# Turned query and key rows split once over 128 partitions, and raw weight quarters held in tiles of the exponentials

## The chip, the cores and the metric

The kernel runs on one core of a Trainium2 chip. The metric is the device time of one execution in microseconds, as the median of several runs. The engines of a core work side by side, each through its own queue in order: TensorE (PE, matmuls and transpositions into PSUM banks), VectorE (DVE), ScalarE (ACT), GpSimd (POOL), and SyncE (SP), which here issues nearly all DMAs. The profile shows one execution.

## The reference

It is one decoder layer on 1024 tokens of width 1024 in float32. One normalised input goes through one projection, whose columns feed two groups of heads. Cut to what matters here:

```
h = rms_norm(x, norm1_w)
da_q, da_k, da_v, dn_qkv, dn_z, dn_a, dn_b = split(h @ w_in)
da_q, da_k = rms_norm(da_q, q_norm_w), rms_norm(da_k, k_norm_w)   # rows of 64
# differential attention, 4 heads, two 64-wide maps per head
a = softmax(q1 k1^T / 8) - lam * softmax(q2 k2^T / 8)             # causal
da_o = rms_norm(a @ v) * (1 - lam_init)
dn_o = rms_norm(gated_delta_rule(conv_silu(dn_qkv), ...)) * silu(dn_z)   # the "scan"
x = x + concat(da_o, dn_o) @ w_out
x = x + relu(rms_norm(x, norm2_w) @ w_up)**2 @ w_down
```

The change touches the projection of `da_q`, `da_k` and `da_v`, and the way in which queries and keys reach the attention.

## The kernel before

**Matmuls in two parts.** A float32 operand is split into a high part, rounded to the format in which PE multiplies fast (`fp32r` in the profile), and a low part, which is the rest. A product is three matmuls: high by high, high by low, low by high. Every weight so passes through `load_unit` (L199 to L215): a DMA brings a raw piece into a tile `wraw` (L211), ACT casts it into the high part `wH` (L213), and another engine, here DVE, subtracts to get the low part `wL` (L214). There are two `wraw` tiles, and a raw tile is free for the next load when its subtraction is done.

**The attention's projection** (`da_units`, L987). The 1536 columns of `da_q`, `da_k` and `da_v` are projected as three *units* of 512 columns (`todo`). The first unit's weights are loaded elsewhere; those of units two and three by `half_w`, in two halves of four quarters each. A half holds 4 of the 8 blocks of 128 rows of the weight; a quarter is one such block, 128 x 512, which comes in two DMAs of 128 KB (two ranges of 256 columns). For each unit the kernel walks over the eight blocks of 128 tokens in pairs: 2 x 24 matmuls `ps_qk` (L1012 to L1014) into two PSUM banks of the pool `pj`, first those of the first half weight for both blocks, then those of the second. At the last pair of a unit, half the next unit's weights are asked for as soon as the matmuls of the first half are written, the other half after those of the second.

**Leaving the bank** (`leave`). ACT copies the finished bank to `qn` with a scale per token (L1040; for unit two in two pieces, L1034 for values and L1035). Only then can PE start on that bank again. POOL, DVE and POOL again form the norm of each row of 64, and DVE scales `qn` with it.

**Turns** (`da_turns`, L957). There are 32, one for each block of tokens and each 256 columns of queries or keys. PE transposes two blocks of 128 x 128 into a bank `ps_qkt` of the pool `px` (L966, L967), so that the two 64-wide maps of a head lie on partitions 0 to 63 and 64 to 127. Then for each of the two maps (`m`) ACT writes the high part of its 64 partitions (L972) and DVE the low part (L973) on the other 64 partitions of the tile `qa`, so that `qa[:, m]` holds both parts of one map over all 128 partitions. One DMA of 256 KB stores the tile to `qk_d` in DRAM (L977). The attention loads keys from there (`load_head`, two tiles `KS` a head) and queries (`load_q`, L1081), also with their halves exchanged (`qb`). The weights of the norms, `qw` and `kw`, scale the turned rows; the profile shows `kw` as `pv`.

**Attention.** For each head and block of queries, `scores` multiplies (L1148, `ps_sc`), takes the negated maximum (DVE, L1153) and the exponential (ACT, L1157) into a tile `pexp` of 128 x 1024, and combines the two maps on DVE (L1167). `values` transposes the result on PE into `ps_at` (L1189), ACT copies it (L1191), and PE multiplies by the values. Four `pexp` tiles stand in the pool `ae`; before the first exponential the same four hold `gb` and `pb` of the scan's preparation (`horner`). A third exponential of each three goes to a pool `be` once the scan is over.

**The scan** runs at the same time, with loads of `pka` (L839), `pkb` (L894) and `zgt` (L896), PE's `ps_A` (L875), and its output on DVE and ACT (L914, L919, L924). `sy` is its copy that PE waits for at L875.

**What sets the order.** All this is written by generators that a planner (`Interleave`, L40) runs by priority: each yields the time from which it can go on, or a bank. The planner keeps its own clock, which goes forward with the matmuls written (`flow.pe`), and a queue for each engine, in which `flow.chain` enters costs such as `act(256)` or `vec(256, 60)`. For a DMA it adds `DMA_T` = 2500 ns. `unit_time` (L771) gives the times at which the four quarters of a half are to be ready; the third and fourth start when the first and second are done:

```
for i in range(4):
    start = flow.now if i < 2 else done[i - 2]
    done.append(flow.chain(("S", 520.0), (eng, rate), start=start + DMA_T))
```

A store is written when the planner's clock has reached its data (`put_off`). The framework's own scheduler then places what is written in each engine's queue; a load whose tile is free early can stand there far ahead of its place in the code. So a changed cost or a changed tile moves other instructions, too.

Of the kernel before, what the change touches and what calls it, by code (L numbers as in the profile page):

```python
# [18 lines left out]
P = 128  # L19
SEQ = 1024  # L20
DM = 1024
KB = DM // P
NT = SEQ // P
# [5 lines left out]
UC = 260  # L29
# [103 lines left out]
def tile_hymba_layer(  # L133
# [6 lines left out]
    nc = tc.nc  # L140
    V, S, G, T = nc.vector, nc.scalar, nc.gpsimd, nc.tensor
# [3 lines left out]
    w_in_v = w_in[0].rearrange("(kb p) c -> p kb c", p=P)  # L145
# [5 lines left out]
    dram = ctx.enter_context(tc.tile_pool(name="dram", bufs=1, space=DRAM))  # L151
# [39 lines left out]
    qk_d = dram.tile([2, 2, NT, P, 2, 2, P], F32, name="qk_d")  # L191
# [4 lines left out]
    hH = hpool.tile([P, KB, SEQ], F32R, name="hH")  # L196
    hL = hpool.tile([P, KB, SEQ], F32R, name="hL")

    def load_unit(src, ranges, k0=0, nk=KB, eng=None, rp=None):  # L199
        eng = eng or G  # L200
        width = sum(n for _, n in ranges)
        wh, wl = staged("wH"), staged("wL")
        wh = wh[:, :nk * width].rearrange("p (k c) -> p k c", k=nk)
        wl = wl[:, :nk * width].rearrange("p (k c) -> p k c", k=nk)
        st = 2 * UC // width
        for k in range(0, nk, st):
            raw = rp.tile([P, 2 * UC], F32, tag="wraw", name="wraw", bufs=5) if rp else laid("wraw")
            raw = raw[:, :st * width].rearrange("p (k c) -> p k c", k=st)
            o = 0
            for c0, n in ranges:  # L210
                nc.sync.dma_start(raw[:, :, o:o + n], src[:, k0 + k:k0 + k + st, c0:c0 + n])  # L211
                o += n
            S.copy(wh[:, k:k + st, :], raw)  # L213
            eng.tensor_tensor(wl[:, k:k + st, :], raw, wh[:, k:k + st, :].bitcast(F32), ALU.subtract)  # L214
        return wh, wl  # L215
# [149 lines left out]
    with tc.manual_schedule(engines={T.engine, V.engine, S.engine}):  # L365
# [49 lines left out]
        raw = n1.tile([P, NT, UC], F32, name="zr")  # L415
# [331 lines left out]
    ae = actx.enter_context(tc.tile_pool(name="ae", bufs=4, **right))  # L747
# [16 lines left out]
    flow = Interleave()  # L764
# [3 lines left out]
    HF = (slice(0, 64), slice(64, 128))  # L768
    MM, TR = 219.0, 110.0

    def unit_time(eng="G", rate=1230.0):  # L771
        done = []
        for i in range(4):
            start = flow.now if i < 2 else done[i - 2]
            done.append(flow.chain(("S", 520.0), (eng, rate), start=start + DMA_T))
        return done

# [176 lines left out]

    late, accs, vts, v_at, qa_free = [], {}, {}, {}, [0.0] * 3

    def da_turns():  # L957
        for i in range(4 * NT):
            while not late:
                yield flow.now + 50, None  # L960
            g, kind, tb, qn, t = late[0]
            r = yield from flow.bank("px", at=max(t + 2000, qa_free[i % 2] - 500))
            late.pop(0)
            pt = px.tile([P, 512], F32, tag="px", name="ps_qkt")
            T.transpose(pt[:, 0:P], qn[:, 0:P], ident)
            T.transpose(pt[:, P:2 * P], qn[:, P:2 * P], ident)  # L966
# [3 lines left out]
            for m in range(2):  # L970
                a, b = HF[m], HF[1 - m]
                S.activation(qa[a, m, :], pt[a, 0:256], AF.Copy, scale=wv[a])  # L972
                V.scalar_tensor_tensor(qa[b, m, :], pt[a, 0:256], wv[a], qa[a, m, :].bitcast(F32),  # L973
                                       ALU.mult, ALU.subtract)
            flow.pe(2 * TR)
            t = flow.chain(act(256), act(256), vec(256, 60), vec(256, 60), start=max(flow.now, qa_free[i % 2]))
            flow.put_off(t, ("qa", i % 2), lambda g=g, kind=kind, tb=tb, qa=qa: nc.sync.dma_start(  # L977
                qk_d[g, kind, tb], qa.bitcast(F32).rearrange("p m (h t) -> p m h t", h=2)))
            qa_free[i % 2] = t + DMA_T
            flow.hold(r, t)  # L980
            state["turned"] += 1
            if state["turned"] % (2 * NT) == 0:
                flow.due(lambda t, key: key[0] == "qa")
                state["da"] += 1
                state["da_t"] = flow.now + 6000
        sdctx.close()
    def da_units():  # L987
        todo = [[(512, 256), (0, 256)], [(1024, 256), (768, 256)], [(1280, 256), (256, 256)]]

        def half_w(src, ranges, k0):  # L990
            return load_unit(src, ranges, k0, 4, eng=V), unit_time("V", 610.0)

        w = [(w, [0.0] * 4) for w in first_w]
        freed = [0.0, 0.0]
        for i in range(3):
            if i == 1:
                vts[0] = ap.tile([P, NT, P], F32, tag="vt", name="vt")
            for pair in range(NT // 2):
                pss = {}
                for kh in range(2):  # L1000
                    (wh, wl), wt = w[kh]
                    for j in range(2):
                        tb = 2 * pair + j
                        sl = slice(tb * P, (tb + 1) * P)
                        if kh == 0:
                            yield max(freed[j], wt[0] if pair == 0 else 0.0), None
                            pss[j] = pj.tile([P, 512], F32, tag="pj", name="ps_qk")
                        ps = pss[j]
                        for k in range(4):
                            if pair == 0 and j == 0:  # L1010
                                yield wt[k], None
                            T.matmul(ps, hH[:, 4 * kh + k, sl], wh[:, k, :], start=(kh + k == 0), stop=False)  # L1012
                            T.matmul(ps, hH[:, 4 * kh + k, sl], wl[:, k, :], start=False, stop=False)  # L1013
                            T.matmul(ps, hL[:, 4 * kh + k, sl], wh[:, k, :], start=False, stop=(kh + k == 4))  # L1014
                            flow.pe(3 * 227)
                            if k < 3 or kh == 0:
                                yield flow.now, None
                        if kh == 1:
                            freed[j] = yield from leave(i, tb, ps)
                    if pair == NT // 2 - 1:  # L1020
                        if i < 2:
                            w[kh] = half_w(w_in_v, todo[i + 1], 4 * kh)
# [41 lines left out]
    def load_head(h, pool):  # L1064
        KS = []
        for m in range(2):
            k = pool.tile([P, SEQ], F32R, tag=f"KS{m}", name=f"KS{m}")
            nc.sync.dma_start(k.bitcast(F32).rearrange("p (b t) -> p b t", t=P),
                              qk_d[h // 2, 1, :, :, m, h % 2, :].rearrange("b p t -> p b t"))
            KS.append(k)  # L1070
        return KS

# [8 lines left out]
    def load_q(h, tb):  # L1081
        qa = ap.tile([P, 2, P], F32R, tag="qa", name="qa", bufs=2)
        qb = ap.tile([P, 2, P], F32R, tag="qb", name="qb", bufs=2)
        src = qk_d[h // 2, 0, tb, :, :, h % 2, :]
# [9 lines left out]
    def scores():  # L1094
        heads, loaded, npe, nsc, since = {}, {}, 0, 0, 0
        while state["da"] < 1:
            yield flow.now + 300, None
        heads[0] = load_head(0, ap), load_v(0, ap)
        q = load_q(*order[0])
        yield state["da_t"] + 3000, None  # L1100
        for u, (h, tb) in enumerate(order):
# [16 lines left out]
            if q is None and h > 0:  # L1118
                q = load_q(h, tb)
# [419 lines left out]
    w = {0: dict(zip("abcd", raws))}  # L1539
# [125 lines left out]
    todo = [(0, 7), (1, 5), (0, 4)]  # L1665
# [189 lines left out]
```

## Time and profile before

| what | value |
| --- | --- |
| median of 3 runs | 1226.64 us (1225.75 to 1227.22) |
| profiled execution, whole | 1226.58 us |
| its span, first to last instruction | 1224.9 us |
| mean granted clock of TensorE in it | 0.998 of full speed |
| busy: PE / DVE / ACT / POOL | 1212.0 / 850.0 / 604.6 / 121.0 us |
| DMA | 199.04 MB, mean 163 GB/s |

In the groups of instructions a row gives line, engine, operation and tiles, then the count, the busy time and the mean of one instruction in ns, and behind the second bar the idle time of the engine just before them, with what ended most of it. In the timeline a row gives start (us from the span's start), duration, engine, line, tiles and shapes, and in brackets how long the engine had waited, and for whom. "x4" in the timeline or in the queues means that like instructions in a row are one row. Line numbers are those of the kernel before.

### The profile page before, as it was taken

How to read it: one execution, taken by the hardware profiler on the slowest of the kernel's cores; microseconds unless marked ns; L12 is line 12 of the kernel's file. 1: busy time of each engine (PE TensorE's matmuls, PEld its weight loads, DVE VectorE, ACT ScalarE, POOL GpSimd, SP SyncE). 2: the span in 40 equal slices, each digit the busy share in tenths (PEclk: the TensorE clock that was granted, in tenths of full speed). 3: DMA queues.
4: the chain of work that ended last, by engine and by line, in shares of the span. 5: the costliest groups of instructions: out<-in, count | busy, mean ns of one | idle time of the engine just before them, and what ended most of it. 6: DMA issues, size and time to landing. Idle time of an engine off the chain costs nothing.

```text
span 1224.9 us, 17632 instructions
## 1 busy us (share of the span) xinstructions
PE 1212.0 (99%) x6330; PEld 1029.2 (84%) x6330; DVE 850.0 (69%) x1448; ACT 604.6 (49%) x1176; POOL 121.0 (10%) x162
## 2 busy tenths in 40 slices
PE   9999999999999999999999999999999999999998
PEld 9988888898888888888788888888888888888887
DVE  7786788477868577766798554566577955786553
ACT  8565545234556555656666444454554333333331
POOL 0011110223332230212100000000000000000000
PEclk9999999999999999999999999999999999999999
DMA  6564442456755584434528433443279855433301
GB/s 230 176 182 125 112 130 87 116 183 218 241 161 180 173 244 135 115 80 142 183 86 291 155 127 133 170 174 135 103 253 353 325 185 183 160 104 104 138 35 69
DMA packets 161087, 199.04 MB, mean 163 GB/s; under 512 B 21008, under 2 KB 120936, under 8 KB 161000
## 3 DMA queue, kind: packets, MB, share of 16 engines
q1 hardware_dynamic: 160856, 197.79, 49.3%
q8 instruction: 50, 0.82, 0.3%
q14 instruction: 37, 0.30, 0.1%
q10 hardware_dynamic: 144, 0.13, 0.0%
HBM read 132.32 MB, written 65.56 MB: 162 GB/s over the span
## 4 chain that ended last, share of the span: by engine, by line
PE 89%; DVE 4%; DMA 3%; ACT 2%; issue 1%; SPq 0%; POOL 0%; ACTq 0%; DVEq 0%
PE X L1454 5%; PE X L1453 5%; PE X L1452 5%; PE X L1768 4%; PE X L1769 4%; PE X L1770 4%; PE ps_dn L221 4%; PE ps_dn L219 4%; PE ps_dn L220 4%; PE ps_qk L1012 3%; PE Y L1454 3%; PE Y L1453 3%; PE Y L1452 3%; PE ps_qk L1014 3%; PE ps_qk L1013 2%; PE ps_o L1201 2%
## 5 line engine op out<-in xcount | busy, mean ns | idle before, releaser
L1371 ACT CAST hH<-ur 128x1024 fp32r<-128x1024 f32 x56 | 58.6, 1048 | 166.0 <-PE X L1769 79.7
L1372 DVE TENSOR_TENSOR hL<-ur,hH 128x1024 fp32r<-128x1024 f32 x56 | 68.5, 1224 | 79.8 <-ACT hH L1371 79.8
L1372 DVE TENSOR_TENSOR op<-raw,op 128x1024 fp32r<-128x1024 f32 x48 | 58.7, 1223 | 75.3 <-PE X L1453 42.3
L1768 PE MATMUL X<-hH 128*128 128x512 f32 x224 | 87.2, 389 | 0.0
L1769 PE MATMUL X<-hL,hH 128*128 128x512 f32 x224 | 87.2, 389 | 0.0
L1770 PE MATMUL X<-hH,hL 128*128 128x512 f32 x224 | 87.2, 389 | 0.0
L1012 PE MATMUL ps_qk<-wH,hH 128*128 128x512 f32 x192 | 82.2, 428 | 1.9 <-ACT qn L1040 1.9
L1014 PE MATMUL ps_qk<-wH,hL 128*128 128x512 f32 x192 | 75.8, 395 | 0.0
L219 PE MATMUL ps_dn<-hH,wH 128*128 128x512 f32 x192 | 75.7, 394 | 0.0
L220 PE MATMUL ps_dn<-hL,wH 128*128 128x512 f32 x192 | 75.6, 394 | 0.0
L1013 PE MATMUL ps_qk<-wL,hH 128*128 128x512 f32 x192 | 75.4, 393 | 0.1
L221 PE MATMUL ps_dn<-hH,wL 128*128 128x512 f32 x192 | 75.4, 393 | 0.0
L1372 DVE TENSOR_TENSOR hL<-dw,hH 128x1024 fp32r<-128x1024 f32 x56 | 68.2, 1220 | 3.2 <-ACT hH L1371 3.2
L1371 ACT CAST op<-raw 128x1024 fp32r<-128x1024 f32 x48 | 50.4, 1050 | 34.8 <-PE Y L1454 20.1
L1371 ACT CAST hH<-dw 128x1024 fp32r<-128x1024 f32 x56 | 58.6, 1047 | 16.7 <-DMA dw<-in_w_down_dram 5.1
L1157 ACT ACTIVATE pexp<-ps_sc,mx 128x128 f32<-128x128 f32 (+7 forms) x64 | 47.3, 740 | 26.1 <-DVE mx L1153 26.1
L595 DVE SCALAR_TENSOR_TENSOR cy<-cp,pv,cy 128x512 f32<-128x512 f32 x72 | 53.7, 750 | 7.8 <-ACT cy L593 7.0
L1153 DVE TENSOR_REDUCE mx<-ps_sc 128x1 f32<-128x128 f32 (+7 forms) x64 | 47.5, 754 | 14.1 <-PE ps_sc L1151 13.5
L1291 PE MATMUL ps_op<-wH,hH 128*128 128x512 f32 x128 | 53.6, 419 | 0.0
L1293 PE MATMUL ps_op<-wH,hL 128*128 128x512 f32 x128 | 50.3, 393 | 0.0
L1292 PE MATMUL ps_op<-wL,hH 128*128 128x512 f32 x128 | 50.0, 391 | 0.0
L1453 PE MATMUL Y<-hL,op 128*128 128x512 f32 x128 | 49.8, 389 | 0.0
(355 smaller groups left out, 3383.8 us busy)
## 6 DMA issues: line engine op xcount, KB each, us to landing
ur<-ud SPq DMA_DIRECT2D x28, 1024.0 KB, 4.9
raw<-in_w_up_dram SPq DMA_DIRECT2D x32, 512.0 KB, 3.7
dw<-in_w_down_dram SPq DMA_DIRECT2D x32, 512.0 KB, 7.2
qk_d<-qa SPq DMA_DIRECT2D x32, 256.0 KB, 3.1
ud<-ua SPq DMA_DIRECT2D x16, 512.0 KB, 4.0
ud<-s SPq DMA_DIRECT2D x16, 512.0 KB, 3.2
wraw<-in_w_in_dram SPq DMA_DIRECT2D x24, 256.0 KB, 3.5
wraw<-in_w_in_dram SPq DMA_DIRECT2D x48, 128.0 KB, 2.9
```

The lines of the kernel that those rows point to most:

```text
L219: T.matmul(ps, lh(k), rh(k), start=(k == 0), stop=False)
L220: T.matmul(ps, lh(k), rl(k), start=False, stop=False)
L221: T.matmul(ps, ll(k), rh(k), start=False, stop=(k == n - 1))
L1012: T.matmul(ps, hH[:, 4 * kh + k, sl], wh[:, k, :], start=(kh + k == 0), stop=False)
L1013: T.matmul(ps, hH[:, 4 * kh + k, sl], wl[:, k, :], start=False, stop=False)
L1014: T.matmul(ps, hL[:, 4 * kh + k, sl], wh[:, k, :], start=False, stop=(kh + k == 4))
L1371: S.copy(dst[0], src)
L1372: V.tensor_tensor(dst[1], src, dst[0].bitcast(F32), ALU.subtract)
L1453: T.matmul(ps, op[0][:, k, cs], h[1][:, k, :], start=False, stop=False, skip_group_check=True)
L1768: T.matmul(o, v[0][:, j, sl], v[2][:, j, c], start=s0, stop=False, skip_group_check=True)
L1769: T.matmul(o, v[0][:, j, sl], v[3][:, j, c], start=False, stop=False, skip_group_check=True)
L1770: T.matmul(o, v[1][:, j, sl], v[2][:, j, c], start=False, stop=s1, skip_group_check=True)
```

## The change

Four edits go together.

1. A turn writes the high part of both maps with one ACT instruction over 128 partitions, `qa[:, 0, :]`, and the low part with one DVE instruction, `qa[:, 1, :]`. Instead of two pairs on 64 partitions there is one pair on 128.
2. `qa` now holds high and low parts apart, and no longer the maps apart. `store_halves` puts them where the attention wants them, in two DMAs of 128 KB: of the four blocks of 64 rows that a turn has in DRAM (map 0, map 1, each with two halves), the high parts go to the first and last, the low parts to the two in the middle. `qk_d` has the map ahead of the partition, and `load_head` and `load_q` read it so. PE gets the same data at the same places.
3. `load_unit` takes a tile `more`, which holds the raw quarters three and four. `half_w` passes one for each half of the second unit, two in all; they are tiles of the pool `ae` with the tag `pexp`. The third unit has none.
4. The planner counts one ACT and one DVE instruction for a turn, and for the halves with `more` all four quarters start at once (`ring`).

```
@@ -188,7 +188,7 @@
     fsg_d = dram.tile([P, 1024], F32, name="fsg_d")
     rt_d = dram.tile([SEQ], F32, name="rt_d")
     cgr_d = dram.tile([HEADS * SEQ], F32, name="cgr_d")
-    qk_d = dram.tile([2, 2, NT, P, 2, 2, P], F32, name="qk_d")
+    qk_d = dram.tile([2, 2, NT, 2, P, 2, P], F32, name="qk_d")
     v_d = dram.tile([NT, P, 3, P], F32, name="v_d")
     acc_d = dram.tile([NT, P, DM], F32, name="acc_d")
     ud = {i: dram.tile([FF // 512, P, 2, 512], F32, name=f"ud{i}") for i in range(1, 8)}
@@ -196,7 +196,7 @@
     hH = hpool.tile([P, KB, SEQ], F32R, name="hH")
     hL = hpool.tile([P, KB, SEQ], F32R, name="hL")
 
-    def load_unit(src, ranges, k0=0, nk=KB, eng=None, rp=None):
+    def load_unit(src, ranges, k0=0, nk=KB, eng=None, rp=None, more=None):
         eng = eng or G
         width = sum(n for _, n in ranges)
         wh, wl = staged("wH"), staged("wL")
@@ -204,7 +204,10 @@
         wl = wl[:, :nk * width].rearrange("p (k c) -> p k c", k=nk)
         st = 2 * UC // width
         for k in range(0, nk, st):
-            raw = rp.tile([P, 2 * UC], F32, tag="wraw", name="wraw", bufs=5) if rp else laid("wraw")
+            if more is not None and k > 1:
+                raw = more[:, 512 * (k - 2):512 * (k - 1)]
+            else:
+                raw = rp.tile([P, 2 * UC], F32, tag="wraw", name="wraw", bufs=5) if rp else laid("wraw")
             raw = raw[:, :st * width].rearrange("p (k c) -> p k c", k=st)
             o = 0
             for c0, n in ranges:
@@ -768,10 +771,10 @@
     HF = (slice(0, 64), slice(64, 128))
     MM, TR = 219.0, 110.0
 
-    def unit_time(eng="G", rate=1230.0):
+    def unit_time(eng="G", rate=1230.0, ring=2):
         done = []
         for i in range(4):
-            start = flow.now if i < 2 else done[i - 2]
+            start = flow.now if i < ring else done[i - 2]
             done.append(flow.chain(("S", 520.0), (eng, rate), start=start + DMA_T))
         return done
 
@@ -954,6 +957,11 @@
 
     late, accs, vts, v_at, qa_free = [], {}, {}, {}, [0.0] * 3
 
+    def store_halves(dst, qa):
+        blocks = dst.rearrange("m (j r) h t -> (m j) r (h t)", j=2)
+        for part, to in ((0, blocks[0:4:3]), (1, blocks[1:3])):
+            nc.sync.dma_start(to, qa[:, part, :].bitcast(F32))
+
     def da_turns():
         for i in range(4 * NT):
             while not late:
@@ -967,15 +975,11 @@
             flow.begun(("qa", i % 2))
             qa = sd.tile([P, 2, 256], F32R, tag="qa", name="qa", bufs=2)
             wv = qw if kind == 0 else kw
-            for m in range(2):
-                a, b = HF[m], HF[1 - m]
-                S.activation(qa[a, m, :], pt[a, 0:256], AF.Copy, scale=wv[a])
-                V.scalar_tensor_tensor(qa[b, m, :], pt[a, 0:256], wv[a], qa[a, m, :].bitcast(F32),
-                                       ALU.mult, ALU.subtract)
+            S.activation(qa[:, 0, :], pt[:, 0:256], AF.Copy, scale=wv)
+            V.scalar_tensor_tensor(qa[:, 1, :], pt[:, 0:256], wv, qa[:, 0, :].bitcast(F32), ALU.mult, ALU.subtract)
             flow.pe(2 * TR)
-            t = flow.chain(act(256), act(256), vec(256, 60), vec(256, 60), start=max(flow.now, qa_free[i % 2]))
-            flow.put_off(t, ("qa", i % 2), lambda g=g, kind=kind, tb=tb, qa=qa: nc.sync.dma_start(
-                qk_d[g, kind, tb], qa.bitcast(F32).rearrange("p m (h t) -> p m h t", h=2)))
+            t = flow.chain(act(256), vec(256, 60), start=max(flow.now, qa_free[i % 2]))
+            flow.put_off(t, ("qa", i % 2), lambda g=g, kind=kind, tb=tb, qa=qa: store_halves(qk_d[g, kind, tb], qa))
             qa_free[i % 2] = t + DMA_T
             flow.hold(r, t)
             state["turned"] += 1
@@ -987,8 +991,8 @@
     def da_units():
         todo = [[(512, 256), (0, 256)], [(1024, 256), (768, 256)], [(1280, 256), (256, 256)]]
 
-        def half_w(src, ranges, k0):
-            return load_unit(src, ranges, k0, 4, eng=V), unit_time("V", 610.0)
+        def half_w(src, ranges, k0, more=None):
+            return load_unit(src, ranges, k0, 4, eng=V, more=more), unit_time("V", 610.0, 2 if more is None else 4)
 
         w = [(w, [0.0] * 4) for w in first_w]
         freed = [0.0, 0.0]
@@ -1019,7 +1023,8 @@
                             freed[j] = yield from leave(i, tb, ps)
                     if pair == NT // 2 - 1:
                         if i < 2:
-                            w[kh] = half_w(w_in_v, todo[i + 1], 4 * kh)
+                            more = ae.tile([P, SEQ], F32, tag="pexp", name="more") if i == 0 else None
+                            w[kh] = half_w(w_in_v, todo[i + 1], 4 * kh, more)
                         elif kh == 0:
                             pre.append(half_w(w_out_v, [(0, 512)], 4))
         pctx.close()
@@ -1066,7 +1071,7 @@
         for m in range(2):
             k = pool.tile([P, SEQ], F32R, tag=f"KS{m}", name=f"KS{m}")
             nc.sync.dma_start(k.bitcast(F32).rearrange("p (b t) -> p b t", t=P),
-                              qk_d[h // 2, 1, :, :, m, h % 2, :].rearrange("b p t -> p b t"))
+                              qk_d[h // 2, 1, :, m, :, h % 2, :].rearrange("b p t -> p b t"))
             KS.append(k)
         return KS
 
@@ -1081,7 +1086,7 @@
     def load_q(h, tb):
         qa = ap.tile([P, 2, P], F32R, tag="qa", name="qa", bufs=2)
         qb = ap.tile([P, 2, P], F32R, tag="qb", name="qb", bufs=2)
-        src = qk_d[h // 2, 0, tb, :, :, h % 2, :]
+        src = qk_d[h // 2, 0, tb, :, :, h % 2, :].rearrange("m p t -> p m t")
         nc.sync.dma_start(qa.bitcast(F32), src)
         nc.sync.dma_start(qb[HF[0]].bitcast(F32), src[HF[1]])
         nc.sync.dma_start(qb[HF[1]].bitcast(F32), src[HF[0]])
```

No matmul is added or taken away. The lines of after stand three to six rows lower: L213 and L211 become L216 and L214, L972 becomes L978, L1040 becomes L1045, L1157 becomes L1162, L1191 becomes L1196, L919 becomes L922, L839, L894 and L896 become L842, L897 and L899.

How the change moves instructions shows at three places. The first is ACT's queue where the second unit's weights are split, shortly ahead of that unit's first matmuls. L213 is the cast of a quarter from `wraw` to `wH`, L972 the high part of a turn (for `pv` or `qw`), L1040 the copy that frees a `pj` bank, L919 the square of the scan's output. Before:

```order
L213 CAST wH_3476<-wraw 128x512 x2
L972 ACTIVATE qa<-ps_qkt,qw 64x256
L1040 ACTIVATE qn<-ps_qk,rt 128x512
L213 CAST wH_3476<-wraw 128x512 x2
L972 ACTIVATE qa<-ps_qkt,pv 64x256
L972 ACTIVATE qa<-ps_qkt,qw 64x256
L972 ACTIVATE qa<-ps_qkt,pv 64x256
L919 ACTIVATE osq,so<-oc,small_73 128x128
L1040 ACTIVATE qn<-ps_qk,rt 128x512
L213 CAST wH_3619<-wraw 128x512
```

Now, with L216, L978, L1045 and L922 for the same lines:

```order
L216 CAST wH_3469<-wraw 128x512 x2
L216 CAST wH_3469<-more 128x512 x2
L978 ACTIVATE qa<-ps_qkt,pv 128x256
L978 ACTIVATE qa<-ps_qkt,qw 128x256
L1045 ACTIVATE qn<-ps_qk,rt 128x512 x2
L216 CAST wH_3577<-wraw 128x512 x2
L216 CAST wH_3577<-more 128x512 x2
L922 ACTIVATE osq,so<-oc,small_73 128x128 x4
```

The four casts of a half now stand together, and the last two copies of the first unit's banks stand together behind the first half's casts and two turn copies, with no square of the scan between them.

The second place is ACT's queue where the third unit's weights come in, at the attention of head 0 (`wH_4395` before and `wH_4378` now are the first half of unit three; L1157, now L1162, is the exponential, its width in the shape; L1191, now L1196, copies the transposed exponentials). Before:

```order
L1157 ACTIVATE pexp,ssum<-ps_sc,mx 128x512 x2
L1207 COPY om<-ps_o 128x128
L213 CAST wH_4395<-wraw 128x512 x2
L1208 ACTIVATE osq_4344,so_4345<-om,ri 128x128
L972 ACTIVATE qa<-ps_qkt,pv 64x256
L1191 COPY at<-ps_at 128x512
L1157 ACTIVATE pexp,ssum<-ps_sc,mx 128x640 x2
L213 CAST wH_4395<-wraw 128x512
```

Now:

```order
L1162 ACTIVATE pexp,ssum<-ps_sc,mx 128x512
L978 ACTIVATE qa<-ps_qkt,pv 128x256
L216 CAST wH_4378<-wraw 128x512 x2
L1196 COPY at<-ps_at 128x512
L978 ACTIVATE qa<-ps_qkt,pv 128x256
L1162 ACTIVATE pexp,ssum<-ps_sc,mx 128x640
L216 CAST wH_4378<-wraw 128x512
L1162 ACTIVATE pexp,ssum<-ps_sc,mx 128x640
L216 CAST wH_4378<-wraw 128x512
L1162 ACTIVATE pexp,ssum<-ps_sc,mx 128x768
```

The third quarter's cast stood behind both exponentials of 640 columns; now it stands between them, and the fourth stands ahead of the first exponential of 768.

The third place is SP's queue in the scan, some 45 us ahead of the second unit's casts. L839 and L894 load the scan's `pka` and `pkb`, L896 its `zgt`. Before:

```order
L839 DMA pka<-park_d 128x384 x4
L894 DMA pkb<-park_d 128x256 x4
L896 DMA zgt<-zg_d 128x512
L894 DMA pkb<-park_d 128x256
L839 DMA pka<-park_d 128x384 x4
L894 DMA pkb<-park_d 128x256 x4
L839 DMA pka<-park_d 128x384 x4
```

Now, with L842, L897 and L899 for these lines, and L214 for the loads of raw quarters:

```order
L842 DMA pka<-park_d 128x384 x4
L897 DMA pkb<-park_d 128x256 x4
L899 DMA zgt<-zg_d 128x512
L897 DMA pkb<-park_d 128x256
L214 DMA more<-in_w_in_dram 128x256 x3
L842 DMA pka<-park_d 128x384 x4
L214 DMA more<-in_w_in_dram 128x256 x5
L897 DMA pkb<-park_d 128x256 x4
```

All eight loads of `more`, for both halves, stand here, three ahead of a group of four `pka` and five behind it.

More of the change, by code (lines that the diff above doesn't have):

```diff
@@ L190, in tile_hymba_layer @@
     cgr_d = dram.tile([HEADS * SEQ], F32, name="cgr_d")
-    qk_d = dram.tile([2, 2, NT, P, 2, 2, P], F32, name="qk_d")
+    qk_d = dram.tile([2, 2, NT, 2, P, 2, P], F32, name="qk_d")
     v_d = dram.tile([NT, P, 3, P], F32, name="v_d")
@@ L206, in load_unit @@
         for k in range(0, nk, st):
-            raw = rp.tile([P, 2 * UC], F32, tag="wraw", name="wraw", bufs=5) if rp else laid("wraw")
+            if more is not None and k > 1:
+                raw = more[:, 512 * (k - 2):512 * (k - 1)]
+            else:
+                raw = rp.tile([P, 2 * UC], F32, tag="wraw", name="wraw", bufs=5) if rp else laid("wraw")
             raw = raw[:, :st * width].rearrange("p (k c) -> p k c", k=st)
@@ L769, in tile_hymba_layer, with unit_time @@
     MM, TR = 219.0, 110.0
-    def unit_time(eng="G", rate=1230.0):
+    def unit_time(eng="G", rate=1230.0, ring=2):
         done = []
         for i in range(4):
-            start = flow.now if i < 2 else done[i - 2]
+            start = flow.now if i < ring else done[i - 2]
             done.append(flow.chain(("S", 520.0), (eng, rate), start=start + DMA_T))
@@ L955, in tile_hymba_layer, with store_halves @@
     late, accs, vts, v_at, qa_free = [], {}, {}, {}, [0.0] * 3
+    def store_halves(dst, qa):
+        blocks = dst.rearrange("m (j r) h t -> (m j) r (h t)", j=2)
+        for part, to in ((0, blocks[0:4:3]), (1, blocks[1:3])):
+            nc.sync.dma_start(to, qa[:, part, :].bitcast(F32))
     def da_turns():
@@ L969, in da_turns @@
             wv = qw if kind == 0 else kw
[L970 to L974, printed above, removed]
+            S.activation(qa[:, 0, :], pt[:, 0:256], AF.Copy, scale=wv)
+            V.scalar_tensor_tensor(qa[:, 1, :], pt[:, 0:256], wv, qa[:, 0, :].bitcast(F32), ALU.mult, ALU.subtract)
             flow.pe(2 * TR)
-            t = flow.chain(act(256), act(256), vec(256, 60), vec(256, 60), start=max(flow.now, qa_free[i % 2]))
-            flow.put_off(t, ("qa", i % 2), lambda g=g, kind=kind, tb=tb, qa=qa: nc.sync.dma_start(
-                qk_d[g, kind, tb], qa.bitcast(F32).rearrange("p m (h t) -> p m h t", h=2)))
+            t = flow.chain(act(256), vec(256, 60), start=max(flow.now, qa_free[i % 2]))
+            flow.put_off(t, ("qa", i % 2), lambda g=g, kind=kind, tb=tb, qa=qa: store_halves(qk_d[g, kind, tb], qa))
             qa_free[i % 2] = t + DMA_T
@@ L1021, in da_units @@
                         if i < 2:
-                            w[kh] = half_w(w_in_v, todo[i + 1], 4 * kh)
+                            more = ae.tile([P, SEQ], F32, tag="pexp", name="more") if i == 0 else None
+                            w[kh] = half_w(w_in_v, todo[i + 1], 4 * kh, more)
                         elif kh == 0:
```

10 lines of the change are left out of this document (5 added, 5 removed).

## The prediction

> **What bounds the kernel now.** I read the page first, then the sums by stretch, then TensorE's waits, then the timeline around the longest of them.
>
> ```profile
> span 1224.9 us, 17632 instructions
> ...
> PE 1212.0 (99%) x6330; PEld 1029.2 (84%) x6330; DVE 850.0 (69%) x1448; ACT 604.6 (49%) x1176; POOL 121.0 (10%) x162
> ...
> PE 89%; DVE 4%; DMA 3%; ACT 2%; issue 1%; SPq 0%; POOL 0%; ACTq 0%; DVEq 0%
> ```
>
> TensorE (PE) is busy for 99% of the span and makes up 89% of the chain that ended last. The change neither adds nor removes a matmul, so it can only act on the 12.9 us in which PE stood idle, and on matmuls that ran slowly. The next rows give window, length, busy time and count of PE, PEld, DVE, ACT and POOL, the granted clock, and DMA.
>
> ```profile
> 306.00:313.00 7.00, 5.09 (x21) 4.17 (x21) 6.75 (x14) 4.77 (x14) 3.05 (x3) 0.76 0.65 195
> 313.00:613.00 300.00, 294.50 (x1691) 253.38 (x1691) 215.13 (x503) 175.99 (x462) 69.75 (x90) 1.00 0.54 165
> 613.00:1224.90 611.90, 608.62 (x2716) 504.83 (x2714) 395.30 (x390) 269.15 (x279) 0.00 (x0) 1.00 0.46 164
> ```
>
> PE's order is the same in both programs before about 262 us and after about 613 us of this span. Between them PE idles 1.9 us in the seven microseconds from 306, where the clock was 0.76, and 5.5 us in the 300 us behind them. TensorE's waits name what ended the longest:
>
> ```profile
> PE ps_qk L1012 <- ACT qn L1040: 1.9, 1, 1.9
> ...
> PE ps_at L1189 <- DVE pexp L1167: 1.0, 1, 1.0
> ```
>
> PE's timeline there:
>
> ```profile
> 306.49 0.39 PE L1014 MATMUL ps_qk<-wH,hL 128*128 128x512 f32 x1
> 308.79 0.50 PE L1012 MATMUL ps_qk<-wH,hH 128*128 128x512 f32 x1 [1.91 <-ACT qn L1040]
> ...
> 310.82 1.91 PE L875 MATMUL ps_A<-sy,pka 128*128 128x128 f32 x8
> ...
> 325.80 1.06 PE L875 MATMUL ps_A<-sy,pka 128*128 128x128 f32 x8
> ```
>
> After an idle 1.91 us the same eight matmuls took 1.91 us that take 1.06 us at full clock. Over the window the lost clock is 0.24 x 7.0 = 1.7 us. The place so costs 1.9 + 1.7 = 3.6 us. What PE waited for was a PSUM bank that ScalarE (ACT) had to empty (L1040). ACT's timeline:
>
> ```profile
> 298.32 0.69 ACT L1040 ACTIVATE qn<-ps_qk,rt 128x512 f32<-128x512 f32 x1 [0.59 <-PE ps_qk L1014]
> 303.87 1.34 ACT L213 CAST wH<-wraw 128x512 fp32r<-128x512 f32 x2 [4.86 <-DMA wraw<-in_w_in_dram]
> ...
> 306.81 0.47 ACT L972 ACTIVATE qa<-ps_qkt,pv 64x256 fp32r<-64x256 f32 x1 [0.87 <-DVE qa L973]
> 307.53 0.40 ACT L919 ACTIVATE osq<-oc,small 128x128 f32<-128x128 f32 x1 [0.25 <-DVE oc L914]
> ...
> 308.05 0.69 ACT L1040 ACTIVATE qn<-ps_qk,rt 128x512 f32<-128x512 f32 x1
> ```
>
> ACT works in order. It stood 4.86 us before a cast of the second unit's third raw quarter, whose load was still under way, and the copy at 308.05 was queued behind the casts and the half-partition copies of the turns. SyncE (SP) shows why the load was late:
>
> ```profile
> 297.99 1.96 SPq L211 DMA_DIRECT2D wraw<-in_w_in_dram  x4
> ...
> 305.24 1.76 SPq L211 DMA_DIRECT2D wraw<-in_w_in_dram  x4
> ```
>
> With two raw buffers, quarters three and four could not be asked for until quarters one and two had been split; the second group of four is the next half unit's.
>
> **The change, part by part.** *Quarters three and four in `more`.* In the new order the eight loads of `more` stand on SP among the scan's loads of about 250 us, and all four casts of a half stand together on ACT. The old row of wait, 4.86 us, has nothing left to wait for there, and only two turn copies stand between these casts and L1040. I take the whole 3.6 us as gone. What is late next is the other half of the unit: its first two quarters still use the old two buffers and go out after the first split, at about 297.6. By the old row (297.99 to 303.87, 5.9 us) they are there at 303.5; the cast (0.62) and the subtraction (0.69) end at 304.8, and behind them VectorE (DVE) has the scan's copy `sy` (0.69), for which PE is due at about 305.3: a wait of 0 to 0.8 us, and I take **+0.3**.
>
> Do the early loads disturb the scan? Rows of DVE and SP:
>
> ```profile
> 248.48 0.70 DVE L802 STREAM_TRANSPOSE lt<-gb 128x512 f32<-128x512 f32 x1
> ```
> ```profile
> 247.13 2.57 SPq L839 DMA_DIRECT2D pka<-park_d  x4
> 251.89 1.74 SPq L894 DMA_DIRECT2D pkb<-park_d  x4
> ```
>
> The tiles of the exponentials come free with the last transposes of `gb`, at 249.2 at the latest. Three loads go ahead of `pka` and five behind it. At some 0.45 us each the five end at 252.0, and `pkb` could not start before 251.9 anyway. The loads have 45 us until the first cast at 295. Both buffers are free again near 308, and the first exponential runs at 337. I cost this at nothing; if the cover were gone, eight issues are 3.6 us of SP.
>
> *The turns.* Per turn two ACT and two DVE instructions on 64 partitions become one each on 128.
>
> ```profile
> L972 ACT ACTIVATE qa<-ps_qkt,pv 64x256 fp32r<-64x256 f32 x32 | 15.0, 468 | 24.1 <-PE ps_qkt L966 12.9 <-DVE qa L973 7.6 <-DMA qk_d<-qa 2.8
> ...
> L1191 ACT COPY at<-ps_at 128x256 f32<-128x256 f32 x8 | 3.0, 376 | 3.0 <-PE ps_at L1189 3.0
> ...
> L824 ACT ACTIVATE lt<-ps_h 64x256 f32<-64x256 f32 x8 | 3.0, 375 | 10.4 <-PE ps_h L816 10.3
> ```
> ```profile
> L973 DVE SCALAR_TENSOR_TENSOR qa<-ps_qkt,pv,qa 64x256 fp32r<-64x256 f32 x32 | 15.4, 483 | 7.5 <-ACT qa L972 6.6
> ```
>
> No row has the new forms. 64 and 128 partitions of 256 columns take 375 and 376 ns on ACT, so I take 468 and 483 ns for them; above, twice that bounds them (no gain), below, half. With 32 pv and 32 qw copies, 32 x 0.47 = 15 us go from ACT and 32 x 0.48 = 15 us from DVE. Neither sets PE's pace, so by themselves they are worth nothing but what PE waits for. One such wait is the 0.95 us at 342.68:
>
> ```profile
> 340.87 1.49 DVE L924 SCALAR_TENSOR_TENSOR oc<-oc,of,zgt 128x128 f32<-128x128 f32 x4
> 342.28 0.34 DVE L1167 SCALAR_TENSOR_TENSOR pexp<-pexp,cf 128x128 f32<-128x128 f32 x1
> ```
>
> There the first combined exponentials (342.28) came after 1.49 us of the scan's output. In the new order the two first exponentials stand next to each other on ACT, without a turn's copy between, and the four `oc` stand ahead of the second maximum. The transposition on PE is as far behind the scores as it was (3.8 us), and I count **-0.9**, between -0.95 and 0.
>
> *Two stores for one.* SP gets 32 more issues, and each store is 128 KB instead of 256.
>
> ```profile
> qk_d<-qa SPq DMA_DIRECT2D x32, 256.0 KB, 3.1
> ...
> wraw<-in_w_in_dram SPq DMA_DIRECT2D x48, 128.0 KB, 2.9
> ```
> ```profile
> PE ps_p L798 <- DMA gb<-fsg_d: 0.4, 1, 0.4
> ```
>
> A turn's chain of 0.47 + 0.48 twice loses one pair, 0.95 us, and gains one issue, about 0.4. It gets no longer: 0. Were SP's wait hidden by nothing, 32 x 0.4 = 13 us is the end above; the longest wait of PE for a load anywhere is the 0.4 us of the last row, so I stay at 0.
>
> *The new order behind it.* The lighter turns let the planner pull work together. One place on PE, at the end of the second unit, is due closer. There the old rows (PE, DVE, SP, ACT) are:
>
> ```profile
> 366.47 0.39 PE L1148 MATMUL ps_sc<-KS,qa 128*128 128x320 f32 x1
> ...
> 367.76 0.69 DVE L214 TENSOR_TENSOR wL<-wraw,wH 128x512 fp32r<-128x512 f32 x1
> ...
> 370.54 0.79 ACT L1157 ACTIVATE pexp<-ps_sc,mx 128x640 f32<-128x640 f32 x1
> ...
> 372.70 0.62 ACT L213 CAST wH<-wraw 128x512 fp32r<-128x512 f32 x1 [1.27 <-DMA wraw<-in_w_in_dram]
> 372.72 0.34 PE L1148 MATMUL ps_sc<-KS,qa 128*128 128x384 f32 x1
> ```
>
> Before, the next scores (384) came 6.25 us after those of 320. Now two transposes and nine ps_qk matmuls stand between, so they come after 1.4 + 0.1 + 9 x 0.23 = 3.6 us, and their second half 0.8 us later, at about 371.1 on the old clock. That half needs the bank of the second 640-wide exponential, and the cast of the third quarter of unit three now stands **ahead** of this exponential on ACT. `more` does not serve unit three. The cast's load goes out behind the first subtraction (about 368.0), lands after the median 2.9 us at 370.9; the cast (0.53 to the next) and the exponential (0.89) end at 372.4. PE waits 1.3 us less slack: I take **+1.2**. With a load of 2 us it is 0.4; with the 5.9 us of row 297.99 it is 4.3.
>
> Of the other waits between 313 and 613 (5.5 - 0.95 = 4.5 us) I have read no sign of a change: 0, within -2 and +2.
>
> **The sum**, against the profiled execution (span 1224.9, whole 1226.58; the median of the runs is 1226.64, so they agree to 0.06): -3.6 + 0.3 - 0.9 + 1.2 = -3.0 us, or **1223.6 us**.
>
> The Trainium skill, "TensorE: Matmul & The Clock Gate", Part 1, says that the array falls to half clock only after at least one idle window of about 3.4 us. Here 1.91 us of idle stood before matmuls at half pace, so the trace does not agree with that length; the page also says that the window runs freely. Only where its length is kept would the slow stretch belong to something else; that is rival C.
>
> **Rivals.** What a measurement of this kernel can tell from no change is about 0.2%, 2.45 us: faster is below 1224.2, slower above 1229.1.
>
> B. *The wait moves to unit three.* The load behind the cast takes 5.9 us instead of 2.9 and PE stands 4.3 us, with 1.7 us of slow clock after it: 6.0 in place of 1.2, so 1228.4. For it: casts on ACT waited 4.86 and 1.27 us for such loads. In the new order the keys of head 1, two loads of 512 KB, run shortly before. Against: the median load is 2.9 us.
>
> C. *The slow clock is not the gap's.* Then 1.7 us stay: 1225.3. Against it: the clock is 1.00 in the stretches around.
>
> D. *The change does not free the bank.* ACT's copy stays behind something else, such as the scan's `osq`, which waited for DVE at 307.53, and the second unit costs 3.6 us as before: -0.9 + 1.2 + 0.3 gives 1227.2. Against it: no cast that waits for a load stands ahead of the copy.
>
> E. *Slower: casts of unit three in front of the attention on ACT, in both halves.* In the second half, too, a cast now stands ahead of the copies of the turned weights. If the loads of both halves take over 5 us, PE pays 6.0 in the first and a gap like the old one, 3.6, in the second: -3.6 - 0.9 + 0.3 + 6.0 + 3.6 = +5.4, 1232.0. It decides from about 4.5 us of landing in both; the one row of 5.9 us speaks for it, the median of 2.9 against.
>
> **Numbers.** My forecast has 0.54, B 0.19, C 0.05, D 0.10, E 0.12. So faster 0.54, same 0.34, slower 0.12. The range reaches from 1220.6 (2 us of other waits gone, and the first 1 us of unit three) to 1229.4 (B with 1 us more); it leaves out E and a little below.
>
> **What would show it.** No PE gap at the start of unit two, and a granted clock of 1.00 there; casts of `more` with no DMA wait before them; the turns at about 0.47 and 0.48 us, 32 each; no gap at the first transposition of exponentials; a gap of about 1 us before the 384-wide scores near 367 us of the new span, ended by ACT's exponential. I am wrong if turns cost twice as much, if a gap over 1.9 us stands elsewhere between 262 and 613, or if the waits there add to over 8 us.

## The result, and the profile after

The changed kernel takes **1254.08 us** (median of 4 runs, 1253.27 to 1255.88) against 1226.72 us before: a ratio of 1.0226, 95% interval 1.021 to 1.0242. That is 27.4 us slower, where 3 us faster was forecast, and above the range and every rival. The profiled execution took 1255.88 us. The head of its page, and the sums by stretch (columns as before: window, length, busy time and count of PE, PEld, DVE, ACT, POOL, granted clock, DMA):

```profile
span 1254.2 us, 17629 instructions
...
PE 1222.0 (97%) x6330; PEld 1035.5 (83%) x6330; DVE 828.6 (66%) x1416; ACT 589.6 (47%) x1144; POOL 123.4 (10%) x162
...
PE 87%; DMA 8%; DVE 2%; issue 1%; ACT 1%; SPq 1%; POOL 0%; ACTq 0%; DVEq 0%; POOLq 0%
```
```profile
0.00:262.00 262.00, 259.82 (x1643) 228.32 (x1643) 196.54 (x448) 134.69 (x371) 32.30 (x53) 1.00 0.51 150
262.00:642.00 380.00, 353.28 (x1974) 301.93 (x1974) 237.41 (x581) 186.25 (x497) 90.59 (x108) 0.97 0.54 156
642.00:1254.20 612.20, 608.92 (x2717) 505.21 (x2715) 394.60 (x390) 268.69 (x278) 0.54 (x1) 1.00 0.46 164
```

The first two stretches of before:

```profile
0.00:262.00 262.00, 259.75 (x1638) 228.07 (x1639) 196.38 (x446) 134.24 (x370) 32.30 (x53) 1.00 0.49 146
262.00:613.00 351.00, 343.59 (x1980) 296.31 (x1979) 258.31 (x614) 201.21 (x530) 88.67 (x109) 1.00 0.56 172
```

In the first 262 us and in the last 612 us PE is as busy as it was. All 29 us lie in the middle stretch, 380 us instead of 351. Over the span, PE's idle time grew from 12.9 to 32.2 us (19.3) and its busy time by 10.0, with a clock of 0.97 in that stretch: as before, matmuls run slowly behind the gaps (eight that take 1.06 us at full clock take 2.07 us behind the gap of 5.33 us, below). TensorE's waits, longest first (total, times, longest):

```profile
PE ps_A L878 <- DVE sy L869: 6.2, 2, 5.3
PE ps_sc L1153 <- ACT pexp L1162: 4.7, 3, 3.7
PE ps_qk L1016 <- ACT qn L1045: 3.9, 2, 3.7
PE ps_tr L253 <- DMA mt<-mixn_d: 3.3, 3, 1.6
PE ps_sc L1153 <- DMA v_d<-qn: 2.7, 1, 2.7
PE ps_o L908 <- DMA pkb<-park_d: 1.8, 3, 1.1
```

No single gap: PE waits for the scan, for exponentials, for banks and for transfers (`mt` with `mixn_d`, `v_d`, `pkb`) that it did not wait for before. What they have in common shows in the chain that ended last, whose DMA share rose from 3% to 8%. Its long pieces in the stretch, in order of time (start, length; some left out):

```profile
263.79 7.32 DMA qk_d<-qa
273.24 7.59 DMA qk_d<-qa
...
285.61 7.50 DMA qk_d<-qa
...
479.53 7.73 DMA qk_d<-qa
...
492.43 7.69 DMA mt<-mixn_d
```

All but the last are stores of the turns: over 7 us from issue until what waited for them went on. The one store of before landed after 2.5 us (median of all 32; the 3.1 of the queues' row covers 9 of them). The last is a load that stands behind a load of keys (512 KB), with no store of high parts under way. ACT's waits for the stores, before and now (total, times, longest), show the same:

```profile
ACT qa L972 <- DMA qk_d<-qa: 2.8, 1, 2.8
```
```profile
ACT qa L978 <- DMA qk_d<-qa: 24.7, 8, 6.6
```

ACT's timeline and, below, PE's show one such wait at work:

```profile
290.51 0.47 ACT L978 ACTIVATE qa<-ps_qkt,pv 128x256 fp32r<-128x256 f32 x1 [6.56 <-DMA qk_d<-qa]
293.62 0.47 ACT L978 ACTIVATE qa<-ps_qkt,qw 128x256 fp32r<-128x256 f32 x1 [2.64 <-DMA qk_d<-qa]
294.00 0.68 ACT L1045 ACTIVATE qn<-ps_qk,rt 128x512 f32<-128x512 f32 x1
```
```profile
294.73 0.50 PE L1016 MATMUL ps_qk<-wH,hH 128*128 128x512 f32 x1 [3.67 <-ACT qn L1045]
```

ACT may not overwrite a turn's tile until its store has landed. Behind it stands the copy that frees PE's bank, as in the gap of before, but with a store in the place of a load. And the loads suffer, too. ACT, DVE and PE in the second half of unit two:

```profile
318.75 1.35 ACT L216 CAST wH<-wraw 128x512 fp32r<-128x512 f32 x2 [6.18 <-DMA wraw<-in_w_in_dram]
```
```profile
319.40 0.69 DVE L217 TENSOR_TENSOR wL<-wraw,wH 128x512 fp32r<-128x512 f32 x1 [4.92 <-ACT wH L216]
320.01 0.68 DVE L869 COPY sy<-ps_A 128x512 f32<-128x512 f32 x1
```
```profile
320.75 2.07 PE L878 MATMUL ps_A<-sy,pka 128*128 128x128 f32 x8 [5.33 <-DVE sy L869]
```

The load of a quarter, asked for at 312.10 us, just behind a store of 311.00, came so late that the scan's copy `sy`, queued on DVE behind the subtraction, kept PE waiting 5.3 us.

At unit three, the place that rival B named, the same happened. ACT and PE:

```profile
389.50 0.62 ACT L216 CAST wH<-wraw 128x512 fp32r<-128x512 f32 x1 [3.82 <-DMA wraw<-in_w_in_dram]
```
```profile
390.95 0.44 PE L1153 MATMUL ps_sc<-KS,qa 128*128 128x384 f32 x1 [3.71 <-ACT pexp L1162]
```

There, too, the load (383.80) was issued behind a store of high parts (382.61).

**Two kinds of store.** Each DMA raises a semaphore when it lands, and the trace records the updates. Counted for the stores of all 32 turns:

| kernel, DMA | updates of its semaphore | issue to the last: median (least to most) |
| --- | --- | --- |
| before, the one store, 256 KB | 16 | 2.5 us (2.0 to 5.6) |
| after, high parts, 128 KB | 3 | 6.2 us (4.6 to 8.1) |
| after, low parts, 128 KB | 16 | 5.7 us (4.3 to 7.7) |

The store of the high parts is another kind: one update about 1 us after the issue, and two late ones. Between 262 and 460 us, all 185 other DMAs had 16, and in 52% of them the last came over 1 us behind the fourteenth (median 1.05 us; before 0.17). The two DMAs of the late quarter above show it one by one: 14 of their 16 updates were there at 315.57 and 315.92 us. The two late ones of the store ahead of them came at 317.23 and 317.36, and only then, at 318.2 to 318.7, the last two of each load. So two of the 16 DMA engines carried the whole high-part store, and what stood behind it on those two came late. The order of SP's instructions tells the difference before any run. The two stores of a turn read there:

```
L963 DMA qk_d<-qa 2x64x256
L963 DMA qk_d<-qa 128x256
```

The high parts go to the first and last of four blocks of 64 rows. With a hole between them the DRAM side can't be one run of 128 rows, and its outermost dimension is 2 (the trace, too, lists the destinations as 2 x 64 and as 128 pieces of 1 KB). The Trainium skill, "DMA: Bandwidth & Descriptors", section "Why a DMA increments its semaphore by 16 and not by 1", states such a rule: the number of engines is the largest up to 16 that divides the slowest dimension of both sides, and the engines left out are made up for in one early update, so 2 engines leave 1 + 2 updates. The trace agrees: 3.

### The profile page after: what moved, and what is told of

Read it like the earlier page. It is cut to its first block, busy times and chain, and to the rows that moved or that the text cites. A ratio compares the mean times of both kernels' runs of the same rounds, so it can differ in the third digit from the quotient of the medians.

```text
span 1254.2 us, 17629 instructions
## 1 busy us (share of the span) xinstructions
PE 1222.0 (97%) x6330; PEld 1035.5 (83%) x6330; DVE 828.6 (66%) x1416; ACT 589.6 (47%) x1144; POOL 123.4 (10%) x162
## 4 chain that ended last, share of the span: by engine, by line
PE 87%; DMA 8%; DVE 2%; issue 1%; ACT 1%; SPq 1%; POOL 0%; ACTq 0%; DVEq 0%; POOLq 0%
PE X L1457 5%; PE X L1458 5%; PE X L1459 5%; PE X L1775 4%; PE X L1774 4%; PE X L1773 4%; DMA qk_d<-qa 4%; PE ps_dn L222 3%; PE ps_dn L223 3%; PE ps_dn L224 3%; PE ps_qk L1016 3%; PE Y L1457 2%; PE Y L1458 2%; PE Y L1459 2%; PE ps_qk L1018 2%; PE ps_qk L1017 2%
## 5 line engine op out<-in xcount | busy, mean ns | idle before, releaser
L1162 ACT ACTIVATE pexp<-ps_sc,mx 128x128 f32<-128x128 f32 (+7 forms) x64 | 47.2, 739 | 24.7 <-DVE mx L1158 24.5
L1457 PE MATMUL Y<-hH,op 128*128 128x512 f32 x128 | 49.8, 389 | 0.0
```

Of the source, the lines that this page charges most:

```text
L1457: T.matmul(ps, op[0][:, k, cs], h[0][:, k, :], start=start and k == 0, stop=False, skip_group_check=True)
```

## The experiments

**Theory N** (narrow): the store of the high parts runs on 2 of 16 engines, and all of the loss follows. **Theory I** (issues): it is the 32 more DMAs on SP and their 1 KB pieces. **Theory M**: it is the quarters in `more`, their early loads or the new order. M holds what the prediction feared (rivals B and E).

**e1.** The two stores by map, 64 partitions each, in place of by part. The halves of the second map change places in DRAM; its score sums the same four products.

```
-        for part, to in ((0, blocks[0:4:3]), (1, blocks[1:3])):
-            nc.sync.dma_start(to, qa[:, part, :].bitcast(F32))
+        for m in range(2):
+            nc.sync.dma_start(dst[m].rearrange("(j r) h t -> r j (h t)", j=2), qa[HF[m]].bitcast(F32))
```

> As the changed kernel, but each of the two stores of a turn takes the 64 partitions of one map, high and low part together, so that the DRAM side begins with 64 rows; count and bytes of the stores are the same. Theory N (the store of the high parts, whose DRAM side is two blocks of 64 rows apart, is served by 2 of the 16 DMA engines and lands after 4 to 7 us; all else follows): the stores land in about 3 us, ACT waits for them under 5 us in all instead of 24.7, and the time is 1221 to 1227 us. Theory I (twice as many issues on SP, 1 KB packets): 1245 us or more, as before this edit. Theory M (the loads of the third and fourth quarters and the new order): 1245 us or more.

**e2.** The changed kernel without its second part:

```
-                            more = ae.tile([P, SEQ], F32, tag="pexp", name="more") if i == 0 else None
+                            more = None
```

> As the changed kernel with its two stores, but no weight quarter goes to a tile of the exponentials; all use the two raw buffers. Theory N and theory I: 1245 to 1262 us, as the changed kernel or up to 5 us above it. Theory M: 1224 to 1230 us.

**e3.** The kernel before with `more`, `load_unit` and `unit_time` as in the change, and nothing else of it.

> The kernel before, with the third and fourth quarters of the second unit in tiles of the exponentials, and its own turns and stores. Theory N and theory I: no loss; 1222 to 1227 us, the gap of 1.9 us ahead of the second unit gone. Theory M: 1240 us or more.

**e4.** The edits of e1 and e2 together.

> The turns of the changed kernel with the stores by map, and no quarter in a tile of the exponentials. Theory N: 1223 to 1229 us, and e1 is 1 to 4 us faster than this. Theory I: 1245 us or more. Theory M: 1224 to 1229 us.

| kernel | turns and stores | quarters in `more` | median, us | to before (95%) |
| --- | --- | --- | --- | --- |
| before, same chip | old, one store | no | 1225.53 | 1 |
| e1 | new, two wide | yes | **1221.12** | 0.9958 (0.9946 to 0.9971) |
| e2 | new, one narrow | no | 1262.38 | 1.0298 (1.0284 to 1.0312) |
| e3 | old, one store | yes | 1226.89 | 1.0008 (0.9999 to 1.0016) |
| e4 | new, two wide | no | 1228.03 | 1.0019 (1.001 to 1.0027) |

Only the narrow store divides the slow kernels from the others. With the same number of stores, bytes and 1 KB pieces e1 is 33 us faster than the changed kernel: I and M fall. e2 is 8 us slower than the changed kernel, where up to 5 were expected, so the quarters in `more` gave some of it back there. e4 is 6.9 us slower than e1, where N expected 1 to 4: two misses of size. In e1 the stores land in 2.5 us, and ACT waits for them 1.8 us in all. ACT's row, the queues' row (count, KB, median to landing) and windows, columns as above:

```profile
ACT qa L977 <- DMA qk_d<-qa: 1.8, 3, 0.9
```
```profile
qk_d<-qa SPq DMA_DIRECT2D x64, 128.0 KB, 2.5
```
```profile
262.00:306.00 44.00, 44.00 (x273) 38.97 (x272) 34.68 (x96) 17.75 (x48) 19.30 (x20) 1.00 0.81 227
306.00:313.00 7.00, 7.00 (x35) 5.76 (x34) 5.82 (x20) 2.90 (x11) 2.76 (x3) 1.00 0.90 267
```

The gap of unit two is gone: PE is busy for all of the seven microseconds in which it stood for 1.9, at full clock. e1 beats both kernels.

**e5 to e8** put the suspect into the kernel before, where nothing else is changed. A turn's own store stays; behind it a second one writes 128 KB to a scratch tensor that nothing reads. Its rows stand close together (e5), or a row is left out after every 64 (e6) or 32 (e7). e6:

```
+    nar_d = dram.tile([2, 2, NT, 2, 65, 256], F32, name="nar_d")
...
+                d = nc.sync.dma_start(qk_d[g, kind, tb], qa.bitcast(F32).rearrange("p m (h t) -> p m h t", h=2))
+                with tc.issue_after(d.ins):
+                    nc.sync.dma_start(nar_d[g, kind, tb][:, 0:64, :], qa[:, 0, :].bitcast(F32))
```

> The kernel before, with a second store for each turn: the high-part columns of its tile, 128 KB, go once more to a scratch tensor in DRAM that nothing reads, whose 128 rows stand close together. Theory N: 0 to 4 us over the kernel before; the second store lands in 2 to 4 us. Theory I: 20 us or more above the kernel before.

> As e5, but the scratch tensor has a row left out after every 64 rows, so that the store has two blocks of 64 rows; bytes, rows and issues are the same. Theory N: its store is served by 2 DMA engines, lands after 4 to 8 us, and the time is 15 to 45 us over e5. Theory I: within 3 us of e5.

> As e5, with a row left out after every 32 rows: four blocks. Theory N: 4 DMA engines, about half the landing time of e6, and a loss over e5 that is under half of that of e6. Theory I: within 3 us of e5.

For e8 the last line reads `hH[:, 0, 0:256]`:

> As e6, but the second store reads a fixed stretch of the normalised input, which nothing rewrites in this stage, so that no turn waits for the buffer that it reads; it still takes its place behind the turn's own store. If the loss of e6 comes from the turns' waits for their buffers (ring of two), this is within 5 us of e5. If it comes from the later transfers that stand behind it on the same two DMA engines, this keeps over half of the loss of e6 over e5.

| kernel | updates | second store lands, median | median, us | over e5 |
| --- | --- | --- | --- | --- |
| e5, close together | 16 | 2.3 us | 1228.15 | |
| e6, two blocks | 3 | 6.3 us | 1262.87 | 34.7 us |
| e7, four blocks | 5 | 4.7 us | 1241.32 | 13.2 us |
| e8, two blocks, other source | 3 | 6.0 us | 1258.55 | 30.4 us |

Before was 1225.92 on the same chip. The same bytes, rows and issues cost 2.2 us in one shape and 36.9 in another, and the updates are the number of blocks plus one. N said "about half the landing time" for four blocks; it is three quarters, a miss, while the loss is 38% of e6's, as expected. e8 keeps 88% of e6's loss although no turn waits for what its second store reads. ACT's waits for stores in e6 and e8 (total, times, longest):

```profile
ACT qa L973 <- DMA nar_d<-qa: 31.8, 10, 5.5
```
```profile
ACT qa L973 <- DMA qk_d<-qa: 15.6, 7, 4.7
```

In e8 it is the turn's own wide store that comes late, behind the narrow store of the turn before it (3.7 us to landing in the median, 2.3 in e5). So the greater part of the loss is what the narrow store does to all transfers behind it. SP itself also stood for the stores in the changed kernel; this row gives its longest such wait in total, at the queries' loads (5.0 us there before):

```profile
SPq L1090 <- DMA qk_d<-qa: 9.4, 2, 5.1
```

What of the loss comes by SP's standing still and what by the two busy engines was not separated.

**e9** tells the shape from the number once more: the blocks of the high-part store go as two DMAs of their own.

> As the changed kernel, with the two blocks of the high-part store sent as two DMAs of 64 rows each, beside the store of the low parts: three stores a turn, 96 in all, each with its rows outermost. Theory N: 1220 to 1226 us, within 3 us of e1, though SP issues 32 more. Theory I (the number of stores counts): 8 us or more over e1.

It took 1223.26 us (0.9982, 0.9973 to 0.9991; before again 1225.53): 96 stores, 2.1 us over e1 with 64, and 31 us under the changed kernel with its 64.

**e10** asks where e1's gain comes from, since neither half has any alone. It is e1 with the planner left at two buffers (`ring=2`).

> As e1, but the planner still counts two buffers for the second unit, so that the third and fourth quarter are planned late and the second half's casts stand behind two squares of the scan on ACT. If the gain of e1 (4.4 us) comes from the earlier loads and the lighter turns themselves, this stays within 1.5 us of e1. If it comes from the order that the planner makes of them, this is 2 us or more over e1, with a wait of TensorE over 1 us near the start of unit two or three.

It took 1224.94 us (0.9998, 0.9989 to 1.0007), 3.8 us over e1, and PE has a wait of 1.9 us at the values' matmuls in unit three (at 390.8 us), ended by a turn, and one of 1.5 before the first transposed exponentials (336.0). Its waits:

```profile
PE ps_o L1205 <- DVE qa L978: 1.9, 1, 1.9
...
PE ps_at L1193 <- DVE pexp L1171: 1.5, 1, 1.5
```

At the start of unit two it has no gap, yet it loses elsewhere what was gained there. So the new order is needed for the gain. e3 and e4 show that the gap of unit two only moves as long as one of the two parts is missing. In e3, with the quarters early and the old turns, PE's timeline has its longest wait 5 us later, for a turn:

```profile
313.94 0.30 PE L968 MATMUL ps_qkt<-ident,qn 128*128 128x128 f32 x1 [2.54 <-DVE qa L976]
```

and in e4, with light turns and late quarters, PE waits for a quarter's cast:

```profile
317.12 0.51 PE L1015 MATMUL ps_qk<-wH,hH 128*128 128x512 f32 x1 [1.58 <-ACT wH L216]
```

## Why the prediction was wrong, step by step

**The step that failed** is *Two stores for one*. It costed the new stores by their bytes and issues: one more issue of 0.4 us against a pair of instructions saved, "0", with 32 x 0.4 = 13 us of SP as the upper end. For the landing it showed only the row of 128 KB loads (2.9 us), though no row shows a transfer whose DRAM side is in two pieces. And it stayed at 0 because PE itself waited for loads 0.4 us at most; the wait came by way of ACT (24.7 us for the stores, 2.8 before) and by later loads. The high-part store lands after 6.2 us and makes what stands behind it late; in place of 0 the term was +33 (e1 against the changed kernel), above the bound that the step gave. The bound was wrong in kind: it counted SP's time, and the cost lay on the DMA engines. The shape `2x64x256` stood in the order of SP. The rule of the Trainium skill named above would have turned it into 2 of 16 engines.

None of the rivals had this cause. B came at its place: it forecast a gap of 4.3 us ahead of the 384-wide scores, and 3.71 us stand there. But they are a small part of the 27 us, and without the narrow store the gap is 0.74 us (e1, below).

**The other steps** can be read in e1, which is the changed kernel without that fault. It was 4.4 us faster than before (forecast: 3.0).

- *Second unit, -3.6:* the gap and the slow clock are gone when both parts are there (windows of e1 above); with the gap the slow clock went, so C falls. By the quarters alone it is not gained: e3 has 1226.89. The step said that only two turn copies would stand between casts and bank; with the old turns, a turn is late next (the row of e3). Why just that turn, was not tried. The sum holds, but not as a term of one edit.
- *Early loads of `more`, 0:* as taken. The five behind `pka` end at 252.1 us in the changed kernel (forecast 252.0), and no wait for `pkb` is among PE's in e1.
- *Second half, +0.3:* 0; `sy` is not among PE's waits of e1.
- *Turns:* 0.47 and 0.48 us, as taken; 32 each with those for `qw`. Groups of the changed kernel, ACT and DVE:

```profile
L978 ACT ACTIVATE qa<-ps_qkt,pv 128x256 fp32r<-128x256 f32 x16 | 7.6, 473 | 34.2 <-PE ps_qkt L974 21.3 <-DMA qk_d<-qa 12.9
...
L979 DVE SCALAR_TENSOR_TENSOR qa<-ps_qkt,pv,qa 128x256 fp32r<-128x256 f32 x16 | 7.7, 480 | 13.2 <-ACT qa L978 11.9 <-DMA zgt<-zg_d 1.2
```

- *First transposition, -0.9:* gone in e1, as forecast.
- *Unit three, +1.2:* there, at the forecast place, 0.74 us. PE and ACT in e1:

```profile
365.74 0.44 PE L1152 MATMUL ps_sc<-KS,qa 128*128 128x384 f32 x1 [0.74 <-ACT pexp L1161]
```
```profile
364.28 0.62 ACT L216 CAST wH<-wraw 128x512 fp32r<-128x512 f32 x1 [0.85 <-DMA wraw<-in_w_in_dram]
364.80 0.79 ACT L1161 ACTIVATE pexp<-ps_sc,mx 128x640 f32<-128x640 f32 x1
```

The cast waited 0.85 us for its load, and the exponential behind it ended the gap. That is the forecast's chain. Its size was in part luck: by the forecast's own rows the load goes out at 368.45 (367.76 + 0.69) and not 368.0, and the scores' second half is due at 370.9 (366.47 + 3.6 + 0.8) and not 371.1, which makes 1.9 us.

## What to carry to other kernels

Before a DMA is costed by its bytes, look at the outermost dimension on both of its sides: two blocks with a hole between them put 128 KB on 2 of 16 engines, and the same rows cut the other way, 64 rows outermost, on all 16. A narrow transfer is not only late itself; it delays the transfers behind it, so its price is to be looked for in waits that name other tensors. And two edits that each give nothing may gain together, when each leaves the other's wait as the next one.

## What the runs showed of the hardware that was not expected

Four blocks took three quarters of the landing time of two (4.7 and 6.3 us against 2.3 on 16 engines), not half: twice the engines bought 1.6 us. The quickest of the 32 stores took 4.80 us in e6, 3.24 in e7 and 1.99 in e5. An estimate from these three: about 1.7 us that every store takes, and 6.2 us divided by the number of engines.

It is the same two engines from one narrow store to the next, as far as the trace tells. In the changed kernel two of them, issued at 284.47 and 285.61 us, landed one behind the other, at 290.06 and 293.11, and the DMAs behind both had two late updates and not four. The share of DMAs with 16 updates whose last one came over 1 us behind the fourteenth was 52% in the changed kernel and 62% in e6, against 12% in e5.
